# Loading the first half of the SSD norm's weight when the rotary angles leave its slot, in a two-layer hybrid decoder kernel

## The chip, the cores and the metric

The kernel runs on one core of a Trainium2 chip. The metric is device time of one launch in microseconds. An execution's time is a little longer than its span, which goes from the first to the last instruction in the trace. A change of 0.2% (2.5 us) is about what a measurement of this kernel can tell from none.

## The reference

Two layers on a sequence of 256 tokens with 1024 channels, all in float32:

```python
for l in range(DEPTH):                     # DEPTH = 2
    h = h + hybrid_mixer(rmsnorm(h, norm_mix_w[l]), ...)
    h = h + swiglu(rmsnorm(h, norm_ffn_w[l]), w_gate_up[l], w_down[l])
return rmsnorm(h, final_norm_w)

# in hybrid_mixer
q, k, v, g_ret, z, xbc, dt, gate_ret, gate_ssd = split(h @ w_in)
qf, kf = rotary(q), rotary(k) * RET_DK ** -0.5          # 4 heads
yr = silu(g_ret) * norm(retention(qf, kf, v))
o_ret = yr @ ret_out                                    # 2048 x 1024
ys = ssd_scan(silu(conv(xbc)), softplus(dt), ...) * silu(z)
ys = group_norm(ys) * ssd_norm_w                        # 2048 weights, 4 groups
o_ssd = ys @ ssd_out
return (sigmoid(gate_ret) * o_ret + sigmoid(gate_ssd) * o_ssd) @ w_o
```

The two things that the change touches are the rotation of q and k by a table of angles, and the multiplication of the SSD branch by `ssd_norm_w`.

## The kernel before

Every weight comes once from HBM in pieces of 128 x 1024 float32 (512 KB). ACT turns a piece into its high part (`wh`, line 506), DVE takes the difference as the low part (`wl`, line 531), and PE multiplies high x high, high x low and low x high (lines 548 to 550, or 1034 and 1037). So each piece passes through SP (the load into one of five `raw` slots, line 486), ACT, DVE and PE.

Part of the products are done in Strassen's manner, with seven products in place of eight: 11, t1, t2, 22, t3, 21 and t4 (`seven` and `out_wino`). The products t1 to t4 need sums of weight blocks. For t3 and t4 a second block is added to the first by a DMA that adds at its destination (line 413, issued by POOL); these are the adding transfers, two for t3 and two for t4 in each such stage. The bank of the product before is copied out by ACT (`copied`: u1 after 11, u2 after t2, u3 after t3), and the next product into the same bank waits for this copy.

A layer's mixer runs in this order: v, the gates' and the B, C, dt columns, then heads of q and k alternating with columns x of the SSD branch, then g (the retention's gate) alternating with x, then the output product of the retention (`ret`, in the profile about 292 to 340 us in layer 0 and 911 to 959 in layer 1), the four columns of z, the output product of the SSD branch (`ssd`), and w_o.

What is issued when is settled while the program is built. Each step is a generator that asks for slots (`Sem`), events and engine time (`Op`); a simulated clock (`Flow`) picks on every engine the ready operation with the least priority number. The outcome is one fixed order of instructions per engine. The chip follows that order, with semaphore waits between the engines.

The slot that matters is `wb`, one buffer of 128 x 1024 (`wbS`, line 265). In each mixer it holds, one after the other: the mixer norm's weight, the rotary angles (`load_angles`, first 512 columns), the first and the second half of the SSD norm's weight (`ssd_w(0)`, `ssd_w(1)`, through `load_wb`, issued by POOL at line 672 as a broadcast to 128 partitions), and the FFN norm's weight. `rotary` gives the slot back when the last of the eight rotations (q and k of four heads) has been done. `z_begins(0)` asks for both halves of the weight when the first z column starts in the planned order; the second half waits for the first to be used up. `z_post` reads them.

Names in the traces: `seg` is the 128 x 8 x 128 tile of the SSD branch's decays, loaded as a broadcast from `acs`; `dec` are the two slots in which the first weight blocks of the retention's product lie; `rr` is the inverse square root of a retention head's mean square, taken on POOL (line 243); `ips` and `yps` are PE's products of the SSD scan; `sx` are buffers for copies of banks.

Of the kernel before, what the change touches and what calls it, by code (L numbers as in the profile page):

```python
# [192 lines left out]
def trunk_kernel(  # L193
# [23 lines left out]
    fl = Flow()  # L217
# [449 lines left out]
    def load_wb(src, pr, eng="pool"):  # L667
        yield wbS

        def emit():  # L670
            w = new_wb()
            (nc.sync if eng == "sp" else nc.gpsimd).dma_start(out=w, in_=src.partition_broadcast(P))
            return w

        w = yield Op(eng, 450 if eng == "sp" else 1050, emit, pr)
        yield fl.transfer(4 * P * D)
        return w
# [633 lines left out]
    def layer(l, mix, nxt, opening=None):  # L1311
# [261 lines left out]
        def load_angles():  # L1573
            if l:
                yield DEC_AT
            yield wbS

            def emit():
                w = new_wb()
                nc.sync.dma_start(out=w[:, : 2 * SEQ], in_=consts[:, K_COS:K_DEC])  # L1580
                return w[:, :SEQ], w[:, SEQ : 2 * SEQ]

            a = yield Op("sp", 450, emit, -1)
            fl.transfer(8 * P * SEQ)
            fl.set(angles, a)

        if l:
            fl.spawn(load_decays())
            fl.spawn(load_angles())
        else:  # L1590
            first_tables.extend([load_angles, load_decays])
# [271 lines left out]
        def ssd_w(i):  # L1863
            w = yield from load_wb(ssd_norm_w[l][i * D : (i + 1) * D], at_job[0])
            fl.set(wbs[i], w)
# [25 lines left out]

        def z_begins(g):
            if g == 0:
                for i in range(2):
                    fl.spawn(ssd_w(i))
            if g == 2:
                fl.spawn(seven_sums(zops, yz, (0, 1), "A", at_job[0] + ZS_PR))

        def z_job(g):
            z_begins(g)  # L1900
            return tm_job(xT, z_post(g))
# [266 lines left out]
    def whole():  # L2168
# [64 lines left out]
        for l in range(DEPTH):  # L2233
            yield from layer(l, norms[l], norms[l + 1], None if l else opening)
# [87 lines left out]
```

## Time and profile before

| | us |
|---|---|
| median of 3 runs | 1253.92 (1253.69 to 1253.99) |
| the profiled execution | 1253.99 |
| its span | 1252.2 |
| PE busy | 1238.6 (99%) |
| DVE busy | 1104.9 (88%) |
| ACT busy | 872.7 (70%) |
| POOL busy | 72.7 (6%) |

Of 266.07 MB moved, 236.93 MB go through queue q1 (SP's) and 27.38 MB through q0 (POOL's). The granted clock of PE was 0.999.

How to read the rows below. A timeline row has the start, the time, the engine, the line, the operation with output and inputs, how many instructions it joins, and in brackets the idle time before it with what ended it. SPq and POOLq rows are DMA issues; a row of DMA issues ends in KB and in the microseconds from issue to landing. A row of waits has the total, the number and the longest. A row of windows has, for a stretch, its length and then for PE, PEld, DVE, ACT and POOL the busy time with the number of instructions, the granted clock, the share of the DMA engines and GB/s. A queue row has packets, MB and its share of the engines' time.

### The profile page before, as it was taken

Reading aid. Unit: us, or ns where it says so; the run is one execution under the profiler, and the core shown is the slowest. Engines: PE = TensorE matmul, PEld = TensorE weight load, DVE = VectorE, ACT = ScalarE, POOL = GpSimd, SP = SyncE. Lnnn points to the kernel's source line nnn. Section 1 sums busy time; section 2 is a strip of 40 time slices with the busy share of each in tenths; the row PEclk is TensorE's granted clock in tenths of the full one; section 3 lists DMA queues with packets and bytes.
Section 4 is the critical chain, followed back from the end, with each engine's and each line's share of the span. In section 5 each row is a group of like instructions: output and inputs, shape, how many; then the busy total and the mean of one; then the engine's idle time right before and its main releaser. Section 6 shows DMA issues by size and latency. Waiting matters only on the chain.

```text
span 1252.2 us, 17656 instructions
## 1 busy us (share of the span) xinstructions
PE 1238.6 (99%) x6293; PEld 1052.0 (84%) x6293; DVE 1104.9 (88%) x1515; ACT 872.7 (70%) x1310; POOL 72.7 (6%) x92
## 2 busy tenths in 40 slices
PE   9999999999999999999999999999999999999997
PEld 7889888888788788888888898888888888888886
DVE  6998888889899978999798978879889998899995
ACT  7967776886766565786586676867957664776863
POOL 0000000001012001001000000000010110010000
PEclk9999999999999999999999999999999999999999
DMA  9658455566777757877776574554676776678871
GB/s 349 234 147 287 149 188 183 166 212 148 259 247 186 236 184 232 300 214 221 242 259 228 141 247 163 174 181 152 235 203 217 237 217 219 218 207 255 295 208 62
DMA packets 76343, 266.07 MB, mean 212 GB/s; under 512 B 8768, under 2 KB 9664, under 8 KB 76256
## 3 DMA queue, kind: packets, MB, share of 16 engines
q1 hardware_dynamic: 68272, 236.93, 54.2%
q0 software_dynamic: 7552, 27.38, 12.0%
q8 instruction: 49, 0.80, 0.3%
q10 hardware_dynamic: 432, 0.66, 0.2%
q14 instruction: 38, 0.31, 0.1%
HBM read 262.76 MB, written 2.16 MB: 212 GB/s over the span
## 4 chain that ended last, share of the span: by engine, by line
PE 69%; issue 2%; DVE 1%; DMA 1%; ACT 1%; POOLq 0%; POOL 0%; DVEq 0%; ACTq 0%
PE acc L548 15%; PE acc L550 15%; PE acc L549 15%; PE acc L1034 12%; PE acc L1037 6%; PE tr L644 2%; DMA raws<-in_w_sw_dram 1%; PE yps L1784 1%; DVE wl L531 1%; ACT wh L506 1%; DVE D L230 0%; PE ips L1771 0%; DVE sx L230 0%; PE tr L1671 0%; PE acc L1500 0%
## 5 line engine op out<-in xcount | busy, mean ns | idle before, releaser
L531 DVE TENSOR_TENSOR wl<-raw,wh 128x1024 fp32r<-128x1024 f32 (+2 forms) x387 | 457.1, 1197 | 42.2 <-ACT wh L506 41.0
L506 ACT ACTIVATE wh<-raw 128x1024 fp32r<-128x1024 f32 (+2 forms) x387 | 395.2, 1037 | 118.5 <-PE acc L550 49.7
L1034 PE MATMUL acc<-xT,wh 128*128 128x512 f32 x960 | 251.0, 395 | 1.0 <-DVE xT L230 1.0
L548 PE MATMUL acc<-wh,xT 128*128 128x512 f32 (+1 forms) x568 | 220.6, 388 | 0.0
L550 PE MATMUL acc<-wh,xT 128*128 128x512 f32 (+1 forms) x568 | 216.1, 380 | 0.0
L549 PE MATMUL acc<-wl,xT 128*128 128x512 f32 (+1 forms) x568 | 215.9, 380 | 0.0
L1034 PEld LDWEIGHTS acc<-xT,wh 128*128 128x128 f32 x960 | 170.3, 189 | 29.6 <-DVE xT L230 1.3
L1037 PEld LDWEIGHTS acc<-xT,wl 128*128 128x128 f32 x960 | 131.8, 190 | 9.9
L1037 PE MATMUL acc<-xT,wl 128*128 128x256 f32 x960 | 136.2, 283 | 0.0
L549 PEld LDWEIGHTS acc<-wl,xT 128*128 128x128 f32 x568 | 106.7, 188 | 20.8 <-issue 1.4
L548 PEld LDWEIGHTS acc<-wh,xT 128*128 128x128 f32 x568 | 106.7, 188 | 20.5 <-issue 1.4
L550 PEld LDWEIGHTS acc<-wh,xT 128*128 128x128 f32 x568 | 106.7, 188 | 19.6
L506 ACT ACTIVATE wh<-raws 128x1024 fp32r<-128x1024 f32 x80 | 83.9, 1057 | 46.9 <-DVE raws L230 16.5
L531 DVE TENSOR_TENSOR wl<-raws,wh 128x1024 fp32r<-128x1024 f32 x80 | 96.6, 1220 | 16.0 <-ACT wh L506 15.7
L548 PE MATMUL acc<-wh,A 128*128 128x512 f32 x224 | 88.6, 395 | 0.0
L550 PE MATMUL acc<-wh,A 128*128 128x512 f32 x224 | 87.6, 391 | 0.0
L549 PE MATMUL acc<-wl,A 128*128 128x512 f32 x224 | 87.2, 389 | 0.0
L233 DVE SCALAR_TENSOR_TENSOR cc<-cc,cv 128x255 f32<-128x255 f32 (+2 forms) x144 | 67.6, 478 | 11.4 <-ACT cc L223 10.3
L550 PEld LDWEIGHTS acc<-wh,A 128*128 128x128 f32 x224 | 42.0, 188 | 9.4 <-DVE A L230 0.5
L223 ACT ACTIVATE sx<-acc 128x512 f32<-128x512 f32 (+1 forms) x62 | 32.5, 525 | 25.0 <-PE acc L1034 14.2
L549 PEld LDWEIGHTS acc<-wl,A 128*128 128x128 f32 x224 | 42.1, 188 | 8.3
L548 PEld LDWEIGHTS acc<-wh,A 128*128 128x128 f32 x224 | 42.1, 188 | 8.4
(202 smaller groups left out, 1992.7 us busy)
## 6 DMA issues: line engine op xcount, KB each, us to landing
raw<-in_w_tm_dram SPq DMA_DIRECT2D x100, 512.0 KB, 4.1
raw<-in_w_fm_dram SPq DMA_DIRECT2D x80, 512.0 KB, 3.9
raw<-in_w_gf_dram SPq DMA_DIRECT2D x40, 512.0 KB, 4.4
raw<-in_w_gate_up_dram SPq DMA_DIRECT2D x32, 512.0 KB, 7.2
raw<-in_w_down_dram SPq DMA_DIRECT2D x28, 512.0 KB, 6.0
raw<-in_w_gr_dram SPq DMA_DIRECT2D x24, 352.0 KB, 4.3
seg<-acs SPq DMA_DIRECT2D x16, 512.0 KB, 5.9
raw<-in_ret_out_dram SPq DMA_DIRECT2D x16, 512.0 KB, 4.2
```

Of the source, the lines that this page charges most:

```text
L223: return Op("act", cost, lambda: nc.scalar.activation(out=out, in_=in_, func=func, **kw), pr, TABLES.get(func))
L233: return Op("dve", 1.04 * n + 130, lambda: nc.vector.scalar_tensor_tensor(out=out, in0=in0, scalar=scalar, in1=in1, op0=op0, op1=op1), pr)
L506: nc.scalar.activation(out=wh[:, :m], in_=raw[:, :m], func=AF.Copy)
L531: nc.vector.tensor_tensor(out=wl[:, :m], in0=raw[:, :m], in1=wh[:, :m].bitcast(F32), op=ALU.subtract)
L548: nc.tensor.matmul(ps, lhsT=lh, rhs=rh, start=first, stop=False, **kw)
L549: nc.tensor.matmul(ps, lhsT=lh, rhs=rl, start=False, stop=False, **kw)
L550: nc.tensor.matmul(ps, lhsT=ll, rhs=rh, start=False, stop=last, **kw)
L644: nc.tensor.transpose(out=ps[:, j * P : (j + 1) * P], in_=src[:, j * P : (j + 1) * P], identity=ident)
L1034: nc.tensor.matmul(box[0], lhsT=wh[:, k, fsl], rhs=x[:, k, :, :], start=(half, k) == (0, 0), stop=(half, k) == (1, 3))
L1037: nc.tensor.matmul(box[0][:, :SEQ], lhsT=wl[:, k, fsl], rhs=xh[:, k, :], start=False, stop=False)
L1784: nc.tensor.matmul(ps[:, i * HD : (i + 1) * HD], lhsT=sg[:, i, :], rhs=xdt[:, i * HD : (i + 1) * HD], start=True, stop=True)
```

## The change

`load_angles` asks for the first half of the SSD norm's weight as soon as it has put the angles into the slot; the request then waits in the slot's list until `rotary` gives the slot back. `z_begins` asks for the second half alone.

```diff
@@ load_angles @@
             a = yield Op("sp", 450, emit, -1)
             fl.transfer(8 * P * SEQ)
             fl.set(angles, a)
+            fl.spawn(ssd_w(0))
@@ z_begins @@
             if g == 0:
-                for i in range(2):
-                    fl.spawn(ssd_w(i))
+                fl.spawn(ssd_w(1))
```

On POOL, in layer 0, between the third head's `rr` and the first z column (the `raw` and `dec` rows are the four adding transfers):

```order
 L243 TENSOR_TENSOR rr_1849<-ms,mhalf 128x2
 L243 TENSOR_TENSOR rr_2095<-ms,mhalf 128x2
-L243 TENSOR_TENSOR rr_2325<-ms,mhalf 128x2
+L672 DMA wb<-in_ssd_norm_w_dram 128x1024
+L243 TENSOR_TENSOR rr_2327<-ms,mhalf 128x2
 L413 DMA raw<-in_w_rw_dram 128x1024 x2
 L413 DMA dec<-in_w_rw_dram 128x1024 x2
-L672 DMA wb<-in_ssd_norm_w_dram 128x1024
 L243 TENSOR_TENSOR rz<-ms,mhalf 128x1 x4
```

The load of `wb` has moved from behind the four adding transfers to ahead of the fourth head's `rr`. Layer 1 shows the same move. No other load changes its place.

On ACT, in the retention's output product of layer 0, the rows around the copies u2 and u3 (the two `sx` rows) stand in the same order in both kernels; these are those of before, with their waits (PE_49, DVE_49 and Activation_49 are waits for an engine, DMAHW and DMASW for a transfer of SP or of POOL):

```order
L506 ACTIVATE wh_3203<-raw_3066 128x1024 [waits DMAHW2_49,PE_49,Activation_49]
L506 ACTIVATE wh_3216<-raw_3156 128x1024 [waits DMAHW4_49,DVE_49,PE_49]
L1748 ACTIVATE seg_3154<-seg_3154,ax_922 128x128 [waits DMAHW3_49]
L223 ACTIVATE sx_3248<-acc_3110 128x512 [waits DVE_49,PE_49]
L506 ACTIVATE wh_3260<-dec_2852 128x1024 [waits DMASW4_49,Activation_49]
L506 ACTIVATE wh_3267<-dec_2854 128x1024 [waits DMASW5_49,PE_49,Activation_49]
L506 ACTIVATE wh_3277<-raw_3162 128x1024 [waits DMAHW5_49,PE_49,Activation_49]
L506 ACTIVATE wh_3284<-raw_3193 128x1024 [waits DMAHW6_49,PE_49,Activation_49]
L223 ACT_TABLE_LOAD
L223 ACTIVATE sx_3292<-acc_3110 128x512 [waits PE_49]
```

None of these rows moved; `raw_3156` is the last retention weight, loaded by SP right behind a `seg` transfer.

## The prediction

> **What bounds the kernel now.** First the page: which engine is never idle.
>
> ```profile
> span 1252.2 us, 17656 instructions
> PE 1238.6 (99%) x6293; PEld 1052.0 (84%) x6293; DVE 1104.9 (88%) x1515; ACT 872.7 (70%) x1310; POOL 72.7 (6%) x92
> ```
>
> PE is busy for 99% of the span, so a change that removes no matmul can win only where PE waits. Second the waits of PE over the whole program, and third the timeline of PE where they lie.
>
> ```profile
> PE acc L548 <- ACT sx L223: 3.7, 5, 0.9
> ```
>
> ```profile
> 320.02 0.50 PE L548 MATMUL acc<-wh,O 128*128 128x512 f32 x1 [0.81 <-ACT sx L223]
> 320.36 0.39 PE L549 MATMUL acc<-wl,O 128*128 128x512 f32 x1
> 320.59 0.39 PE L550 MATMUL acc<-wh,O 128*128 128x512 f32 x1
> ...
> 326.67 0.50 PE L548 MATMUL acc<-wh,Y 128*128 128x512 f32 x1 [0.91 <-ACT sx L223]
> ```
>
> ```profile
> 938.83 0.50 PE L548 MATMUL acc<-wh,O 128*128 128x512 f32 x1 [0.55 <-ACT sx L223]
> ...
> 945.48 0.50 PE L548 MATMUL acc<-wh,Y 128*128 128x512 f32 x1 [0.92 <-ACT sx L223]
> ```
>
> Four of the five waits stand in the retention's output product, two in each layer: the products t3 and t4 wait until ACT has copied the bank of the product before (u2, u3). A matmul is shown 0.39 us long but the next starts 0.23 after it, so each wait costs 0.16 more than its bracket: 0.97 and 1.07 in layer 0, 0.71 and 1.08 in layer 1, 3.83 us together. That is the most that this stage can give. Why ACT is late stands in its own timeline:
>
> ```profile
> 312.02 1.06 ACT L506 ACTIVATE wh<-raw 128x1024 fp32r<-128x1024 f32 x1 [1.17 <-PE acc L550]
> 316.08 1.06 ACT L506 ACTIVATE wh<-raw 128x1024 fp32r<-128x1024 f32 x1 [3.00 <-DMA raw<-in_w_rw_dram]
> 317.05 2.44 ACT L1748 ACTIVATE seg<-seg,ax 128x128 f32<-128x128 f32 x8
> 319.39 0.57 ACT L223 ACTIVATE sx<-acc 128x512 f32<-128x512 f32 x1
> 319.87 2.00 ACT L506 ACTIVATE wh<-dec 128x1024 fp32r<-128x1024 f32 x2
> 321.77 1.99 ACT L506 ACTIVATE wh<-raw 128x1024 fp32r<-128x1024 f32 x2
> 323.78 1.28 ACT L223 ACT_TABLE_LOAD   x1
> ...
> 326.04 0.58 ACT L223 ACTIVATE sx<-acc 128x512 f32<-128x512 f32 x1
> ```
>
> ```profile
> 934.89 1.06 ACT L506 ACTIVATE wh<-raw 128x1024 fp32r<-128x1024 f32 x1 [2.74 <-DMA raw<-in_w_rw_dram]
> ```
>
> ACT stands 3.00 us (2.74 in layer 1) for one load of retention weights and then works without a gap through both copies, 319.39 and 326.04, that PE waits for. So whatever this load gains, ACT gains, and PE gains up to its two waits. Fourth, who shares the DMA engines with that load:
>
> ```profile
> 305.49 0.89 POOL L672 DMA_DIRECT2D wb<-in_ssd_norm_w_dram  x1
> ```
>
> ```profile
> 305.55 0.33 SPq L1737 DMA_DIRECT2D seg<-acs  x1
> 305.98 0.46 SPq L486 DMA_DIRECT2D raw<-in_w_rw_dram  x1
> ```
>
> ```profile
> wb<-in_ssd_norm_w_dram POOLq DMA_DIRECT2D x1, 512.0 KB, 10.3
> raw<-in_w_rw_dram SPq DMA_DIRECT2D x1, 512.0 KB, 10.0
> ```
>
> ```profile
> seg<-acs SPq DMA_DIRECT2D x1, 512.0 KB, 7.9
> ```
>
> The load is issued at 305.98 and lands 10.0 us later, at 316.0, the moment when ACT starts. The norm's weight, wb, lands at 305.49 + 10.3 = 315.8, just ahead of it. Nobody needs wb then; its first reader on DVE is far behind:
>
> ```profile
> L233 DVE SCALAR_TENSOR_TENSOR sil<-sil,rz,wb x8: 746/748/752, 349.0 to 390.1; 128x512 f32<-128x512 f32 x8
> ```
>
> **The change, its gain.** It takes 512 KB (0.524 MB) out of the burst. How long they hold the load up is read from the two queues, q0 (POOL's) and q1 (SP's), first from 304 to 312.3, then from 312.3 to 315.3.
>
> ```profile
> q0 software_dynamic: 267, 1.03, 71.7%
> ```
>
> ```profile
> q0 software_dynamic: 161, 0.54, 46.3%
> ```
>
> ```profile
> 312.30:315.30 3.00, 3.00 (x22) 2.73 (x21) 2.00 (x3) 0.78 (x1) 0.00 (x0) 1.00 1.00 399
> 316.00:320.00 4.00, 3.21 (x14) 2.27 (x13) 2.42 (x3) 3.92 (x11) 0.00 (x0) 1.00 1.03 419
> ```
>
> Up to 312.3, q0 has moved 1.03 MB, the two adding transfers. The 0.54 MB after that are wb; the rest that moves in the same three microseconds (399 GB/s in all, 1.20 MB) is q1's, the end of the seg transfer and our load. The engines' share, ahead of the rate, is 1.00, so they have no gap: every byte of wb is time that q1 would have had. Without wb, q1's bytes end earlier by 0.524 MB at 399 GB/s (1.31 us) or at the 419 GB/s that q1 reaches alone (1.25 us). Layer 1 has the same transfers in the same order and nearly the same wait, so it counts the same. Sum over both layers: 2.50 to 2.62 us; I take 2.6, the end from the burst itself, which is the nearest row.
>
> [...]
>
> Is all of it handed on to PE? After the shift ACT starts the late conversion near 314.8. The seg transfer, first in q1, has landed by 305.55 + 7.9 = 313.5, and PE releases the next wh buffer six matmuls (1.4 us) after the release at 312.02, at 313.4, so neither takes over. Copy u2 then ends near 318.7, ahead of PE, which is free at 320.02 - 0.97 = 319.05: the first wait goes entirely. Copy u3 ends near 325.3, while PE, 0.97 earlier, is free at 324.63: of the second wait some 0.7 us stay. The two together give the 1.3 us, not 2.04, because the ACT chain is the later end. In layer 1 the same: 0.71 goes, 0.5 to 0.6 of the second's 1.08 goes. What is late next is ACT's own list (table load, seg), not a DMA.
>
> **The change, its cost.** The issue moves on POOL ahead of the fourth head's power and of the four adding transfers; on the other engines no instruction changes its place. The stretch it moves to:
>
> ```profile
> 194.77 0.69 POOL L243 TENSOR_TENSOR rr<-ms,mhalf 128x2 f32<-128x2 f32 x1 [21.04 <-DVE ms L238]
> 220.84 0.69 POOL L243 TENSOR_TENSOR rr<-ms,mhalf 128x2 f32<-128x2 f32 x1 [25.38 <-DVE ms L238]
> ```
>
> ```profile
> 200.60 0.69 DVE L230 TENSOR_TENSOR cc<-cc,wb 128x512 f32<-128x512 f32 x1
> ...
> 205.87 0.69 DVE L230 TENSOR_TENSOR xdt<-xdt,sr 128x512 f32<-128x512 f32 x1
> ```
>
> ```profile
> 207.02 1.02 PE L1771 MATMUL ips<-xdt,cbm 128*128 128x512 f32 x2
> ```
>
> The added wait on POOL is for the last rotary product that reads the slot, over at 201.29. Behind it in POOL's queue stands only the power at 220.84, which itself hangs on that head's rotation; 0.89 us of issue fit into a free stretch of 25 us. Cost nothing. SP's queue is not touched, since POOL issues the transfer. On the DMA engines it meets weight loads:
>
> ```profile
> 189.11 11.93 SPq L486 DMA_DIRECT2D raw<-in_w_tm_dram  x4
> ```
>
> ```profile
> raw<-in_w_tm_dram SPq DMA_DIRECT2D x1, 512.0 KB, 3.4
> ```
>
> ```profile
> 214.67 1.06 ACT L506 ACTIVATE wh<-raw 128x1024 fp32r<-128x1024 f32 x1 [1.74 <-PE acc L550]
> ```
>
> The fourth of these loads is issued by 201.04, lands by 204.4 and is converted at 214.67, where ACT waits for PE and not for it. A delay of 1.3 us leaves 9 us of cover. Cost 0; the upper bound, with the cover gone, would be 1.3 per layer. The later parts of the program follow PE and move with it.
>
> Total: 1253.99 us of the profiled execution (span 1252.2; the median of the runs is 1253.92, 0.07 lower) less 2.6: 1251.3 from the median.
>
> **The rivals.** *DVE pays at the new place.* POOL's 0.89 us of issuing now fall into DVE's work between the two rows above, and the product at 205.87 ends at 206.56, only 0.46 ahead of the matmul at 207.02. If DVE stood while POOL issues, PE would lose 0.43 per layer, the gain would fall to 1.7 and the time be 1252.2. Against it: beside the issue at 305.49 DVE's conversions keep their pace,
>
> ```profile
> 304.58 2.35 DVE L531 TENSOR_TENSOR wl<-raw,wh 128x1024 fp32r<-128x1024 f32 x2
> ...
> 323.61 2.35 DVE L531 TENSOR_TENSOR wl<-raw,wh 128x1024 fp32r<-128x1024 f32 x2
> ```
>
> two in 2.35 us, as at 323.61 with POOL idle. [...] Chance 0.07.
>
> *Slower, by the same place.* Each microsecond that DVE loses there beyond 0.46 costs PE one in both layers. From 1.75 us the gain is gone, from 3.0 the kernel is slower by 0.2%. That would need DVE held up to the transfer's landing too: 0.89 + 3.4 = 4.3 us gives 2 x 3.8 - 2.6 = +5.1, 1259. Chance 0.04.
>
> *Nothing moves.* If the load's 10.0 us came from the two adding transfers alone, or another wait took ACT's place at 316, the time would be 1253.9. For it: q0 with the adding transfers holds most of the engines until 312.3. Against it: after that only wb shares them. Chance 0.10.
>
> *All four waits go.* If the load lands 2 us or more earlier (wb's packets slowing others beyond their bytes), the cap of 3.83 holds: 1250.1. Against it: the share of 1.00 leaves no hidden gap. Chance 0.07.
>
> **How the numbers follow.** My forecast, 2.2 to 2.9 us less, has 0.72, with 1251.3 as its middle. The range reaches from the cap, 1250.1, to 1252.9, which takes in the loss on DVE and a gain in one layer only (1252.6); left out are "nothing" and "slower", 0.14. A fifth of a per cent, about what a measurement can tell from no change, is 2.51 us, and my bounds of 2.50 to 2.62 lie at that line: of the forecast's 0.72 I count 0.45 above it. With the cap's 0.07 that is 0.52 for faster; 0.27 + 0.10 + 0.07 = 0.44 for the same; 0.04 for slower.
>
> **What would show it.** In the profile after: wb issued by POOL near 201, and 619 us later (934.89 - 316.08) in layer 1; the load of retention weights landing in about 8.7 us and ACT's wait for it 1.7 and 1.5 us; PE's wait at t3 gone, at t4 still there at some 0.6 us by its bracket; DVE and PE near 207 unchanged. I am wrong if ACT's wait stays at 3.0 (wb was not the cause), if it shrinks and PE's waits stay (another wait behind it), or if a wait for DVE appears at the ips matmul.

## The result, and the profile after

The changed kernel takes 1251.12 us (median of 16 runs, 1250.38 to 1255.18) against 1253.85 us for the kernel before beside it (16 runs, 1253.11 to 1254.99). The ratio is 0.9979, 95% interval [0.9971, 0.9986]: 2.7 us less, and by the interval between 1.8 and 3.6.

The head of the page of the changed kernel, and of its table of PE's waits the rows for the copies and for the opening (total, number, longest):

```profile
span 1250.4 us, 17658 instructions
PE 1237.9 (99%) x6293; PEld 1051.6 (84%) x6293; DVE 1104.9 (88%) x1515; ACT 872.8 (70%) x1310; POOL 72.8 (6%) x92
```

```profile
PE acc L548 <- ACT sx L223: 1.5, 4, 0.6
...
PE tr L644 <- DVE sil L233: 1.2, 1, 1.2
```

PE's waits for ACT's copies fell from 3.7 to 1.5 us; of the 1.5, 0.80 stand in the two retention stages (0.54 and 0.26, rows below), the rest in two waits outside them. The second row is a wait in the opening, ahead of everything that the change touches; it was 0.3 in the profile of before. So this profiled execution enters the retention 0.8 us late, and its span is only 1.8 us shorter. What the stage itself gave is read from distances inside it.

First the new place: POOL's issues in both layers, the landing of the first, and DVE and PE behind it (the `xdt` product feeds the `ips` matmul):

```profile
202.37 0.60 POOL L672 DMA_DIRECT2D wb<-in_ssd_norm_w_dram  x1 [6.14 <-DVE cc L230]
221.62 0.71 POOL L243 TENSOR_TENSOR rr<-ms,mhalf 128x2 f32<-128x2 f32 x1 [18.65 <-DVE ms L238]
```

```profile
820.00 0.60 POOL L672 DMA_DIRECT2D wb<-in_ssd_norm_w_dram  x1 [6.14 <-DVE cc L230]
```

```profile
wb<-in_ssd_norm_w_dram POOLq DMA_DIRECT2D x1, 512.0 KB, 5.0
```

```profile
201.37 0.70 DVE L230 TENSOR_TENSOR cc<-cc,wb 128x512 f32<-128x512 f32 x1
...
202.63 0.70 DVE L230 TENSOR_TENSOR tail<-C,prm 128x512 f32<-128x512 f32 x1
...
206.63 0.70 DVE L230 TENSOR_TENSOR xdt<-xdt,sr 128x512 f32<-128x512 f32 x1
```

```profile
207.80 1.02 PE L1772 MATMUL ips<-xdt,cbm 128*128 128x512 f32 x2
```

POOL issues at 202.37, 0.30 after the last rotary product that reads the slot has ended (201.37 + 0.70 = 202.07). A DVE product that runs beside the issue (202.63) takes 0.70 us like the one ahead of it, the `xdt` product ends at 207.33, 0.47 before its matmul, and that matmul shows no wait. The next POOL instruction still waits for DVE. The transfer that `wb` holds up here is not the `in_w_tm_dram` load that the prediction named (3.4 us in both profiles) but the `in_w_fm_dram` load issued behind it, which lands after 4.5 us where it took 3.1. Nobody pays for that here: PE has no wait from 195 to 225 us in either profile, and ACT's conversions at 202.46 and 214.67 before, 203.24 and 215.44 after, lie as far apart as they did.

Then the old place: the load of retention weights (issued at 306.71), ACT's wait for it in the two layers with the two copies behind it, and PE at t3 and t4:

```profile
raw<-in_w_rw_dram SPq DMA_DIRECT2D x1, 512.0 KB, 8.5
```

```profile
315.34 1.06 ACT L506 ACTIVATE wh<-raw 128x1024 fp32r<-128x1024 f32 x1 [1.52 <-DMA raw<-in_w_rw_dram]
...
318.65 0.57 ACT L223 ACTIVATE sx<-acc 128x512 f32<-128x512 f32 x1
...
325.30 0.58 ACT L223 ACTIVATE sx<-acc 128x512 f32<-128x512 f32 x1
```

```profile
932.72 1.06 ACT L506 ACTIVATE wh<-raw 128x1024 fp32r<-128x1024 f32 x1 [1.24 <-DMA raw<-in_w_rw_dram]
```

```profile
319.56 0.39 PE L550 MATMUL acc<-wh,O 128*128 128x512 f32 x1
319.78 0.39 PE L548 MATMUL acc<-wh,O 128*128 128x512 f32 x1
```

```profile
325.92 0.50 PE L548 MATMUL acc<-wh,Y 128*128 128x512 f32 x1 [0.54 <-ACT sx L223]
```

```profile
943.30 0.50 PE L548 MATMUL acc<-wh,Y 128*128 128x512 f32 x1 [0.26 <-ACT sx L223]
```

The load lands after 8.5 us instead of 10.0 (in layer 1 8.2 instead of 9.7). ACT's wait is 1.52 instead of 3.00 (1.24 instead of 2.74). At t3 PE goes on at its usual 0.22 (319.78 against 319.56), since the copy has ended at 318.65 + 0.57 = 319.22; the wait at t4 stays, smaller. From the `ips` matmul to the start of t4 the stage took 326.67 - 207.02 = 119.65 us; now 325.92 - 207.80 = 118.12: **1.53 us less** in layer 0. In layer 1, counted from a POOL issue of the same stage (911.41 before, 910.76 after, rows below), it took 34.07 and now 32.54: again 1.53.

### The profile page after: what moved, and what is told of

The parts are those of the page before. It is cut to its first block, busy times and chain, and to the rows that moved or that the text cites. A ratio compares the mean times of both kernels' runs of the same rounds, so it can differ in the third digit from the quotient of the medians.

```text
span 1250.4 us, 17658 instructions
## 1 busy us (share of the span) xinstructions
PE 1237.9 (99%) x6293; PEld 1051.6 (84%) x6293; DVE 1104.9 (88%) x1515; ACT 872.8 (70%) x1310; POOL 72.8 (6%) x92
## 4 chain that ended last, share of the span: by engine, by line
PE 93%; issue 2%; DVE 2%; DMA 1%; ACT 1%; POOL 0%; SPq 0%; POOLq 0%; ACTq 0%; DVEq 0%
PE acc L548 19%; PE acc L550 19%; PE acc L549 19%; PE acc L1034 18%; PE acc L1037 9%; PE tr L644 2%; PE yps L1785 2%; DVE wl L531 1%; DMA raw<-in_w_v_dram 1%; PE tr L1672 1%; PE acc L1500 1%; PE ips L1772 1%; PE y L549 0%; PE y L548 0%; PE y L550 0%
```

## The experiments

The theory: the norm's weight held up the retention load by its bytes, ACT handed the delay on, and PE paid at t3 and t4. The rivals: the gain comes from the new place rather than from leaving the old; it comes from the transfer's presence (its issue, its entry in POOL's queue) and not its size; the new place costs something that the gain hides. All edits but one are made to the changed kernel.

**In layer 0 alone.**

```diff
-            fl.spawn(ssd_w(0))
+            if not l:
+                fl.spawn(ssd_w(0))
@@ z_begins @@
             if g == 0:
+                if l:
+                    fl.spawn(ssd_w(0))
```

> The early load in layer 0 alone; layer 1 loads the weight in the old place. Burst theory (the 512 KB beside the adding transfers hold up the last retention weight): half of the gain, 1.5 us under the kernel before (about 1252.4); the load lands in 8.5 us in layer 0 and 9.7 to 10.0 in layer 1; PE waits once in layer 0's retention (0.5 by its bracket) and twice in layer 1's (0.55, 0.9). Rival (the difference lies at the start of the program or in run-to-run scatter): no half step, and waits not split by layer.

Measured: 1252.9 us (11 runs) against 1254.12, ratio 0.9993 [0.9984, 1.0002]. By time this is no proof, since the interval reaches 1. The profile parts the layers cleanly. PE's waits from 300 to 345 us and from 918 to 960 us:

```profile
PE acc L548 <- ACT sx L223: 0.4, 1, 0.4
```

```profile
PE acc L548 <- ACT sx L223: 1.4, 2, 0.9
```

Layer 0 has one wait, as after the change; layer 1 has its two, as before it. The effect is local to each layer's stage.

**The same bytes put back.** The weight is loaded early, and in the old place POOL loads the same 512 KB into the same slot again.

```diff
+        def again(pr):
+            w = yield wbs[0]
+            yield Op("pool", 1050, lambda: nc.gpsimd.dma_start(
+                out=w[:128], in_=ssd_norm_w[l][0:D].partition_broadcast(128)), pr)
@@ z_begins @@
             if g == 0:
+                fl.spawn(again(at_job[0]))
```

> As the changed kernel, and the same 512 KB are loaded a second time into the same slot in the old place, behind the four adding transfers. Burst theory: the gain is gone, 1253.9, the load of retention weights lands in 10.0 us again and PE waits four times. Rival (what helps is the early place itself, or POOL's order): stays at 1251.1.

Measured: 1254.21 us against 1254.12, ratio 1.0003 [0.9994, 1.0011]. The whole gain is gone. Its transfers in the burst in layer 0, and PE's waits over the program:

```profile
wb<-in_ssd_norm_w_dram POOLq DMA_DIRECT2D x1, 512.0 KB, 10.4
...
raw<-in_w_rw_dram SPq DMA_DIRECT2D x1, 512.0 KB, 9.8
```

```profile
PE acc L548 <- ACT sx L223: 3.7, 6, 0.9
```

The sum is that of before (3.7), and the four waits in the two stages are back (0.59 and 0.92 in layer 0, 0.53 and 0.92 in layer 1). So the early place gives nothing by itself; the gain is the old place left free.

**Half of it put back, on half of the partitions.** As above, with `w[:64]` and `partition_broadcast(64)`: 256 KB.

> As the run before, but the second load goes to 64 partitions only: 256 KB with rows of the same size. Bytes theory: half of the hold-up comes back, the load lands in 9.2 to 9.3 us, 1.5 us under the kernel before (1252.4). Rival (an entry in POOL's queue costs as such, whatever its bytes): lands in 10.0, 1253.9.

Measured: 1254.26 us against 1254.12, ratio 1.0002 [0.9994, 1.0011]: half of the bytes took away all of the gain, against the 1252.4 expected. The load lands after 10.2 us in layer 0 and 9.8 in layer 1 (with all 128 partitions 9.8 and 9.7). Each row is a microsecond, with the share of the DMA engines and GB/s at its end, here first and then with all 128 partitions:

```profile
313.00:314.00 1.00, 1.00 (x6) 0.83 (x5) 0.96 (x3) 0.75 (x1) 0.00 (x0) 1.00 1.08 266
314.00:315.00 1.00, 1.00 (x9) 0.89 (x7) 1.00 (x1) 0.00 (x0) 0.00 (x0) 1.00 1.04 250
```

```profile
313.00:314.00 1.00, 1.00 (x8) 0.88 (x7) 1.00 (x1) 0.00 (x0) 0.00 (x0) 1.00 1.02 422
314.00:315.00 1.00, 1.00 (x11) 1.00 (x11) 0.16 (x1) 0.00 (x0) 0.00 (x0) 1.00 0.99 402
```

The engines are as busy (1.08 and 1.04 against 1.02 and 0.99), but only 250 to 266 GB/s move instead of 402 to 422. In this run the stage comes 0.85 us later than in the other, and the first row may still hold the end of the adding transfers, the second of which lands at 314.28 (312.84 in the other run) and beside which, with SP's transfers, only 270 to 295 GB/s move at about a full share (270 at 1.04 from 310 to 312 in the kernel before, 295 at 0.96 from 311 to 312 in the other run); but from 315 to 316, behind them, it is 332 GB/s against 434, and in layer 1 the rate falls too (258 and 352 from 933 to 935, against 422 and 430 from 932 to 934). So this was no half dose in time, and it can't tell bytes from presence. Why the rate falls at an unchanged share no row shows.

**Half of it put back, on all partitions.** As above, with `out=w[:, :512]` and `ssd_norm_w[l][0:512].partition_broadcast(P)`: 256 KB in rows of 2 KB.

> As the changed kernel, and half of the weight (128 partitions x 512 columns, 256 KB, rows of 2 KB) is loaded again in the old place; all 128 partitions are written, unlike in the run with 64. Bytes theory: the load of retention weights lands in 9.2 us, half of the gain is left, 1.5 us under the kernel before. Rival (an entry in POOL's queue costs whatever its bytes): 10.0 us and no gain.

Measured: 1253.17 us (11 runs) against 1254.26, ratio 0.9991 [0.9982, 1.0]. The load (the same in both layers), and PE's waits in the two stages:

```profile
raw<-in_w_rw_dram SPq DMA_DIRECT2D x1, 512.0 KB, 8.9
```

```profile
PE acc L548 <- ACT sx L223: 0.9, 1, 0.9
```

The row of the waits reads the same in both stages: the wait at t3 stays away, and t4's is back to its size before. Nothing, 256 KB and 512 KB in the old place give ratios of 0.9979, 0.9991 and 1.0003. The middle one lies half-way, but its interval reaches from near the one to near the other, so the time alone does not show a half step. Nor do the rows of layer 0: the run with the new place loaded twice (below), which has nothing in the old place, shows 8.9 us and a wait of 0.89 there too, in a profile where SP's issue of the load took 1.16 us and not 0.44.

Layer 1 does separate them. There the load lands after 8.2 to 8.4 us in the four profiles with nothing in the old place (the change twice, the late load by SP, the new place twice), after 8.9 here, and after 9.6 to 9.7 in the three with 512 KB (the kernel before, the change in layer 0 alone, the same bytes put back). From POOL's issue to t4, the distance used above, it takes 32.48 to 32.78 us, then 33.24, then 33.96 to 34.07. So the loss goes with the bytes, about half for half; a price for the mere presence of a transfer would have taken all of it. That rests on one profile for the half, which the times allow and do not prove.

**Neither early nor in the burst.** SP loads the weight late, behind the first loads of the next stage.

```diff
-            fl.spawn(ssd_w(0))
@@ z_begins @@
+        def ssd_w_late(pr):
+            yield wbS
+            yield 6000.0
...
+                nc.sync.dma_start(out=w, in_=ssd_norm_w[l][0:D].partition_broadcast(P))
```

> The first half of the weight is loaded neither early nor in the burst, but after it, by SP behind nine weight loads of the z columns. Burst theory: the same gain as the change, 1251.1, the load lands in 8.5 us, PE waits at t4 alone; the early place costs nothing, so the two agree within 0.5 us. Rival (being early matters): 1253.9. If SP's queue becomes late by this transfer, a wait of ACT for a w_tm load shows near 335.

Measured: 1251.45 us (11 runs) against 1254.12, ratio 0.9979 [0.9971, 0.9988], as the change. Its issue, and the load it no longer disturbs:

```profile
336.81 0.42 SPq L1898 DMA_DIRECT2D wb<-in_ssd_norm_w_dram  x1
```

```profile
raw<-in_w_rw_dram SPq DMA_DIRECT2D x1, 512.0 KB, 8.4
```

SP's queue did not become late by it: ACT's wait for an `in_w_tm_dram` load behind this issue is 2.90 us (at 340.00), where the changed kernel has 3.57 (at 340.26); a wait of 1.43 at 336.04 lies ahead of the issue. So a late place outside the burst does as well as the early one, which speaks against the first rival a second time.

**The new place loaded twice.** After the early load the same 512 KB once more.

```diff
             w = yield from load_wb(ssd_norm_w[l][i * D : (i + 1) * D], at_job[0])
+            if i == 0:
+                yield Op("pool", 1050, lambda: nc.gpsimd.dma_start(
+                    out=w, in_=ssd_norm_w[l][0:D].partition_broadcast(P)), at_job[0])
```

> The changed kernel with the 512 KB loaded twice in the new place, the second time as soon as the first has landed (near 207 us). It prices the new place. Theory: no cost, 1251.1 within 0.5; DVE's steps near 201 to 210 as long as before and no PE wait near 207. Rival (POOL's issue or the landing slows DVE there): 0.4 us or more per layer, 1252 or above, with a PE wait for DVE at the ips matmul.

Measured: 1251.92 us (11 runs) against 1254.26, ratio 0.998 [0.9972, 0.9989]. POOL's two issues:

```profile
201.94 0.60 POOL L672 DMA_DIRECT2D wb<-in_ssd_norm_w_dram  x1 [6.13 <-DVE cc L230]
207.31 0.54 POOL L1867 DMA_DIRECT2D wb<-in_ssd_norm_w_dram  x1 [4.77 <-DMA wb<-in_ssd_norm_w_dram]
```

Doubling the bytes there costs nothing that can be measured, and PE has no wait from 195 to 225 us. The second issue waited for the first to land and so came after the `xdt` product; for DVE ahead of 207 this run doubles nothing, and there the rows of the changed kernel stand alone.

**The other neighbour moved instead.** A transfer can also be taken out of the load's way by order. In the kernel before, the load is issued ahead of the `seg` transfer of 512 KB that stood right before it in SP's queue, and nothing else is changed:

```diff
                 queue.dma_start(out=raw[:, : k * n], in_=src)
+                while behind:
+                    behind.pop()()
...
-                nc.sync.dma_start(out=sg, in_=dr[t, g * HPG : (g + 1) * HPG, :].partition_broadcast(P))
+                def dma():
+                    nc.sync.dma_start(out=sg, in_=dr[t, g * HPG : (g + 1) * HPG, :].partition_broadcast(P))
+                if (g, t) == (3, 0):
+                    behind.append(dma)
+                else:
+                    dma()
```

> The kernel before, weight in the burst, with the same exchange on SP. Theory: the load is ahead of seg in SP's queue and shares the engines with the adding transfers and the weight; it lands near 8.5 us, seg near 10.3; ACT's seg steps start 1.0 us earlier per layer, 2.0 us under the kernel before. Rival: seg now waits out the same burst and nothing is gained, 1254.0.

Measured: 1251.19 us (12 runs) against 1254.26, ratio 0.9977 [0.9968, 0.9987]: 3.1 us less (1.6 to 4.0 by the interval) where 2.0 were expected, so as much as the change, with the norm's weight left where it was. The profile is of the longest of the twelve runs (1255.43 us), whose `ips` starts at 211.48 and so 4.5 us late; only distances inside the stage are read from it. Its transfers in layer 0, and what ACT waits for now:

```profile
raw<-in_w_rw_dram SPq DMA_DIRECT2D x1, 512.0 KB, 8.0
seg<-acs SPq DMA_DIRECT2D x1, 512.0 KB, 10.0
```

```profile
318.04 1.06 ACT L509 ACTIVATE wh<-raw 128x1024 fp32r<-128x1024 f32 x1 [0.54 <-DMA raw<-in_w_rw_dram]
320.37 2.45 ACT L1758 ACTIVATE seg<-seg,ax 128x128 f32<-128x128 f32 x8 [1.27 <-DMA seg<-acs]
```

The load lands at 8.0 and the `seg` transfer takes the 10.0. Part of ACT's wait has moved to `seg`: 1.27 us (0.64 in layer 1). PE's wait at t3 is gone in both layers, t4's stays at 0.94 in layer 0 and is gone in layer 1. By the distances used above layer 0 is 1.13 us shorter than before and layer 1 1.75.

**Both.** The same exchange in the changed kernel.

> The changed kernel with two neighbours on SP exchanged: the last load of retention weights goes ahead of the seg transfer, not behind it. Theory (ACT's late conversion is set by that load's place in the burst, and the PE waits by ACT): the load lands near 7.3 us after its issue, ACT starts when PE frees the buffer (0.1 to 0.4 us of DMA wait instead of 1.5), then waits for seg, which lands about 1.2 us later than now; the seg steps start 1.0 us earlier than in the changed kernel and the two last waits in the retention (0.5 and 0.3 by their brackets) go: 1.1 us under the changed kernel, 3.8 under the one before. Rival (seg takes over as the wait, in full): the same time as the changed kernel.

Measured: 1250.28 us (5 runs) against 1254.26, ratio 0.9966 [0.9955, 0.9978]. In layer 0:

```profile
314.17 1.06 ACT L509 ACTIVATE wh<-raw 128x1024 fp32r<-128x1024 f32 x1 [0.49 <-DMA raw<-in_w_rw_dram]
315.38 2.45 ACT L1759 ACTIVATE seg<-seg,ax 128x128 f32<-128x128 f32 x8 [0.15 <-DMA seg<-acs]
```

The load landed after 8.0 us in layer 0 (7.2 in layer 1), where 7.3 was expected. With the norm's weight away, the `seg` transfer costs ACT only 0.15, and PE's table of waits for the two stages is empty; t4 still starts 0.37 behind the matmul ahead of it and not 0.23, just as the copy ends (325.22 and 325.17 in layer 0), so a last 0.14 is left in each layer. The gains don't add (2.7 and 3.1 us apart, 4.0 together, by the medians), and the waits show why: both are paid out of the same four. By the distances the two layers are shorter by 3.06 us with the change, 2.88 with the exchange and 3.89 with both.

Once more, beside the changed kernel on one chip, to see whether this version is ahead of it:

> The changed kernel once more, beside the next one on one chip. The theory (the load of retention weights is held up by the norm's weight; PE keeps one wait for ACT in each layer) expects the ratio of before, 0.997 to 0.999, and the landing of the load 8.2 to 8.9 us.

> The changed kernel with the last load of retention weights issued ahead of the seg transfer of its job (nothing else differs from the kernel beside it). If both holders-up, the norm's weight and the seg transfer, act through the same two waits of PE, what is left of the waits in the changed kernel, 0.54 and 0.26 us by their brackets and about 0.3 more for each, goes too: 1.4 us less than the kernel beside it, ratio 0.9965 to 0.998 against the kernel before. The rival, that the seg transfer now lands late and ACT waits for it instead, expects the two kernels within 0.5 us.

Measured: the change 1251.52 us (7 runs), ratio 0.9973 [0.9963, 0.9984]; with the exchange 1250.53 us (5 runs), 0.9964 [0.995, 0.9977]. The version with both is 1.0 us lower, less than the 1.4 expected. Of the 35 pairs of runs it is lower in 31, while the intervals against the kernel before overlap: ahead very likely, by about a microsecond.

The change's second profile opens like that of before (`ips` at 206.82, where it was 207.02):

```profile
206.82 1.02 PE L1772 MATMUL ips<-xdt,cbm 128*128 128x512 f32 x2
```

```profile
raw<-in_w_rw_dram SPq DMA_DIRECT2D x1, 512.0 KB, 8.2
```

```profile
324.58 0.50 PE L548 MATMUL acc<-wh,Y 128*128 128x512 f32 x1 [0.17 <-ACT sx L223]
```

From `ips` to t4 it takes 117.76 us, 1.89 less than before, and its span is 1248.5. So the stage's gain is 1.5 to 1.9 us in single executions. The first profile's small difference of spans is accounted for: of the 3.06 us of the two stages 0.78 was lost in the opening and 0.48 behind the stages (584.74 us from one stage to the other before, 584.84 after; 306.72 from layer 1's t4 to the end before, 307.10 after), which leaves the 1.8. In that last stretch the change's profile has a wait of PE for a copy by ACT, 0.2 us between 1010 and 1035, which the profile before lacks. It isn't the change's doing as far as the profiles show: the second one lacks it too, and the run with the same bytes put back, which has no gain, shows 0.3 there.

## Why the prediction was right

Forecast 1251.3, measured 1251.12; a gain of 2.6 us against 2.7. The steps in their order:

- *The wait and its cause.* Right: the load's landing, ACT's wait and PE's waits moved together, came back together with the bytes (1.0003), and with half of them came about half back in layer 1's profile (33.24 us between 32.5 and 34.0), which the time (0.9991) allows.
- *t3's wait goes, t4's stays.* Right. t4's rest was put at 0.6 us by its bracket; it is 0.54 and 0.26 here, 0.17 in the second profile.
- *The cost of the new place.* Right: nothing, by the rows near 207, by the double load (0.998) and by the run without an early load (0.9979). Only the neighbour was the wrong one there: held up was the `in_w_fm_dram` load (3.1 to 4.5 us) and not `in_w_tm_dram`, and nobody waited for it. So the rival of DVE held up beside the issue and its slower form find no support in this place: 0.70 us beside the issue and without.
- *The sizes.* Here the working was short, twice. The load's gain was put at 1.25 to 1.31 us per layer; its landing moved by 1.5 (10.0 to 8.5, 9.7 to 8.2), ACT's wait was put at 1.7 and 1.5 and was 1.52 and 1.24, and the stage gained 1.53 in each layer. The queues show where most of the rest lies: the kernel before from the end of the adding transfers to the load's landing, 312.3 to 316.0, and then the changed one over the same stretch, 313.03 to 315.21:

```profile
q1 hardware_dynamic: 262, 0.94, 62.6%
q0 software_dynamic: 165, 0.54, 37.6%
```

```profile
q1 hardware_dynamic: 245, 0.87, 98.5%
```

Both move some 400 GB/s (1.48 MB in 3.70 us, 0.87 in 2.18). The 0.54 MB are 1.35 us of the difference; the other 0.07 MB, 0.17 us, were SP's own. Which of its transfers they belong to these rows don't tell; the load that was issued next can't be told from ours. That part stays open.

- *What a wait of PE costs.* It was put at the bracket and 0.16 more. The starts of the first matmul behind t3 that reads `Y`, with the POOL issue of layer 1 from which its distance is counted, before:

```profile
322.88 0.39 PE L548 MATMUL acc<-wh,Y 128*128 128x512 f32 x1
```

```profile
911.41 0.90 POOL L413 DMA_DIRECT2D raw<-in_w_rw_dram  x1 [70.78 <-DVE dec L230]
```

```profile
941.68 0.39 PE L548 MATMUL acc<-wh,Y 128*128 128x512 f32 x1
```

and after:

```profile
322.50 0.39 PE L548 MATMUL acc<-wh,Y 128*128 128x512 f32 x1
```

```profile
910.76 0.89 POOL L413 DMA_DIRECT2D raw<-in_w_rw_dram  x1 [70.77 <-DVE dec L230]
```

```profile
940.16 0.39 PE L548 MATMUL acc<-wh,Y 128*128 128x512 f32 x1
```

Without t3's wait layer 0 is 115.86 - 114.70 = 1.16 us shorter up to there, with a bracket of 0.81; layer 1 is 30.27 - 29.40 = 0.87 shorter, with 0.55. A wait costs its bracket and a good 0.3. Part of what was missed stood in the quoted rows: the matmul behind a wait starts its follower 0.34 later (320.02 to 320.36) and not 0.23. So t3 gave 2.03 us in the two layers and t4 1.03 (brackets 0.91 to 0.54 and 0.92 to 0.26), 3.06 in all in that profile, and by this price the cap was nearer to 4.4 than to 3.83: the version with both edits is past the forecast cap by its medians (4.0 and 4.2 us below the kernel before) and by the distances up to t4 alone (3.89), though the intervals of its times take in 3.83.

That the forecast hit the median within 0.2 us is in part luck: its terms were too small (3.06 us in the stages of the first profile, and 3.48 = 1.89 + 1.59 in the second), and the runs gave 2.7 (1.8 to 3.6). In the first profile the difference is the opening and the wait behind the stages, neither of which the forecast counted; for the other runs, which left no profile, it stays open.

## What to carry to other kernels

When an engine stands for one load, list every transfer whose issue-to-landing stretch overlaps that load's, and ask of each when its reader needs it: a transfer without haste was worth its bytes at the measured rate, and a little more (1.53 us a layer in the first profile, where 512 KB at 399 to 419 GB/s are 1.25 to 1.31), when it was moved to a stretch with slack, early or late (ratio 0.9979 both times), and much the same gain was had by exchanging two neighbours in a queue. Follow the gain to the waits that pay it out, since two such edits share one purse (2.7 and 3.1 us alone, 4.0 together). Price a wait of PE by the distance between fixed points around it and not by its bracket, and compare stages rather than spans where the opening of a profile differs.

## What was not expected of the hardware

A broadcast of 256 KB to 64 partitions held up the load beside it as long as one of 512 KB to 128: the share of the DMA engines stayed near 1.0 (1.08 and 1.04 against 1.02 and 0.99 from 313 to 315), the rate fell from 402 to 422 GB/s to 250 to 266, and the load landed after 10.2 us in layer 0 and 9.8 in layer 1 (9.8 and 9.7 beside the 512 KB), where 256 KB to 128 partitions let it land after 8.9 in both.
